# Storing expert 6's result in nine parts on one queue instead of three parts on two

## The chip, the cores and the metric

The kernel runs on one core of one Trainium2 chip. The metric is device time in microseconds (us): the time of one execution of the program, taken as the median of several runs. The core has TensorE (matrix products), VectorE (DVE in the profile), ScalarE (ACT), GpSimd (POOL) and SyncE (SP). GpSimd, SyncE and ScalarE can issue DMAs, each on a queue of its own; 16 DMA engines carry out what is in these queues.

## The reference

Eight experts, each with its own 256 x 512 input and its own two-layer network:

```
x  [8, 256, 512]    w1 [8, 512, 2048]    b1 [8, 2048]
                    w2 [8, 2048, 512]    b2 [8, 512]        all float32

h   = max(x @ w1 + b1, 0)          # per expert, 256 x 2048
out = h @ w2 + b2                  # per expert, 256 x 512, float32
```

The output is 8 x 256 x 512 float32, 4.19 MB. The weights are 67 MB; they are cast to float16 while they are loaded.

## The kernel before

**Loads.** GpSimd issues all weight loads, one DMA of 128 partitions per expert and matrix (`load_w1`, `load_w2`; the last two experts' `w2` in two halves), in a fixed order that the list `ring` writes out. Three buffers each hold `w1` and `w2`; a load waits until the expert that used its buffer is done. SyncE loads the inputs of experts 0 and 1 at the start, as two DMAs of 128 rows of 4 KB; GpSimd loads the others.

**Products.** The loop over `s` runs `first_product(s)` and, three experts behind, `second_product(s - 3)`. The first gives h transposed, 16 blocks of 128 rows, which ScalarE takes out of PSUM with bias and ReLU. The second accumulates two PSUM tiles `po` of 128 x 512, one for the even and one for the odd ones of the 256 output rows, and starts with a product of ones and `b2`.

**Results.** In `store`, VectorE copies the first tile out of PSUM (line 156) and ScalarE the second (line 157), both into an SBUF tile of 128 partitions. Partition p holds the output rows 2p and 2p + 1, so each partition is one contiguous piece of 4 KB in SBUF and in HBM. Below, "row" means such a 4 KB piece. Three ways lead to HBM:

- Experts 0 to 3 share one tile (`GROUPS`), stored by one GpSimd DMA of 2 MB; experts 4 and 5 share another, stored by one of 1 MB. `flush` (line 140) issues both late, after the last weight loads. They are called group 0's and group 4's store here.
- Expert 7 is stored by one SyncE DMA of 128 rows, after its two copies.
- Expert 6 is stored in the parts that the table `PARTS` gives: first row, last row, and whether ScalarE (true) or SyncE (false) issues it. This is line 164, in the loop at the end of `store`.

**Waiting.** A DMA raises a semaphore of its own when it has landed. The framework gives each DMA of SyncE and ScalarE the next of eight semaphores in turn, and gives GpSimd's another eight. At the end of the program SyncE waits for all of them, one instruction after the other (shown under line 261).

Of the kernel before, what the change touches and what calls it, by code (L numbers as in the profile page):

```python
# [10 lines left out]
def kernel(  # L11
# [12 lines left out]
    E, T, H = x.shape  # L24
# [12 lines left out]
    HALVED = (E - 2, E - 1)  # L37


    PARTS = {E - 2: ((0, 25, False), (25, 121, True), (121, 128, False))}  # L40
    nXF32 = 2
    X_LOADS = {2: 2, 4: 4}

# [98 lines left out]
    def store(e, po):  # L142
# [16 lines left out]
        if e in group_of:  # L159
            if e == first + n - 1:  # L160
                pending[first] = (dst, out_sb)
            return
        for p0, p1, scalar in PARTS.get(e, ((0, P, False),)):
            (nc.scalar if scalar else nc.sync).dma_start(out=dst[p0:p1], in_=out_sb[p0:p1])
# [101 lines left out]
```

## Time and profile before

| what | time |
|---|---|
| median of 3 runs | 181.49 us (181.38 to 181.49) |
| span of the profiled execution, first to last instruction | 179.7 us |
| that execution's own device time | not recorded apart from the span |
| difference between the median and the span | 1.8 us |
| TensorE busy | 129.1 us, 72% of the span |
| GpSimd's DMA queue, share of the 16 engines' time | 96.6% |
| second products of experts 5, 6, 7 start | 149.5, 158.7, 166.3 us |
| group 0's store issued / landed | 148.3 / 175.1 us |
| group 4's store issued / landed | 159.7 / 177.5 us |
| expert 6's store issued | 166.4 us |
| expert 7's last copy ends, its store is issued | 173.9 us |
| expert 7's store landed | 178.8 us |

The profile is of one execution. Its times are counted from the first instruction. A DMA instruction on an issuing engine's queue takes a fraction of a microsecond; the data moves afterwards on the DMA engines, and the time to landing is the time from the start of the issue to the last increment of the semaphore. The page counts a DMA's packets: one per piece of data and one for each engine's increment of the semaphore. The column PEq, SPq and so on means an engine's sequencer or DMA queue.

### The profile page before, as it was taken

The numbers are of one execution on the slowest core, as the hardware profiler recorded it, in microseconds if no ns is written. First come the engines' busy times: TensorE is split into PE (matmuls) and PEld (weight loads), VectorE is DVE, ScalarE is ACT, GpSimd is POOL, SyncE is SP. The second block draws the span as 40 slices with busy tenths as digits, with TensorE's granted clock in tenths as the row PEclk, the third lists the DMA queues.
The fourth block names the chain that finished last, engine by engine and source line by source line (L and its number), as shares of the span: only waits on it lengthen the run. The fifth ranks groups of instructions, "written<-read, shape, count | busy, mean of one in ns | idle before, by whom it ended". The sixth has DMA issues, their size and how long they took to land.

```text
span 179.7 us, 1958 instructions
## 1 busy us (share of the span) xinstructions
PE 129.1 (72%) x784; PEld 85.8 (48%) x784; DVE 88.0 (49%) x125; ACT 70.2 (39%) x151; POOL 13.1 (7%) x28
## 2 busy tenths in 40 slices
PE   0005099969595970899969597969497887999950
PEld 0004079969592320795369244844195332433420
DVE  0999942987000199999999998003200020301010
ACT  0000459969593022483099005950586020020010
POOL 7000002120201010001010001000200021010000
PEclk9999999999998798589999889999999996999996
DMA  5999999999999999999999999999999999999996
GB/s 216 251 226 199 233 212 197 233 224 193 228 230 192 221 233 215 197 230 230 204 208 230 219 193 233 226 193 222 230 215 197 233 206 204 223 212 215 335 420 250
DMA packets 3829, 40.56 MB, mean 226 GB/s; under 512 B 461, under 2 KB 477, under 8 KB 1133
## 3 DMA queue, kind: packets, MB, share of 16 engines
q0 software_dynamic: 3232, 38.35, 96.6%
q1 hardware_dynamic: 476, 1.70, 2.4%
q10 hardware_dynamic: 112, 0.39, 0.5%
q8 instruction: 6, 0.10, 0.2%
q14 instruction: 3, 0.02, 0.0%
HBM read 71.39 MB, written 4.19 MB: 421 GB/s over the span
## 4 chain that ended last, share of the span: by engine, by line
DMA 66%; PE 26%; POOL 2%; another core or an unknown queue 1%; issue 1%; ACT 0%; POOLq 0%
DMA w1sb<-in_w_dram 44%; DMA w2sb<-in_w_dram 22%; PE po L178 18%; PE ph L121 8%; PE po L171 1%; POOL w1sb L84 1%; ACT out L157 0%; POOL x L76 0%; POOL b_sb L192 0%; POOL b_rows L196 0%; POOLq L250 0%
## 5 line engine op out<-in xcount | busy, mean ns | idle before, releaser
L121 PE MATMUL ph<-xT,w1sb 128*128 128x256 f16 x512 | 63.6, 289 | 34.8 <-DMA w1sb<-in_w_dram 23.9
L121 PEld LDWEIGHTS <-w1sb 128*128 128x128 f16 x512 | 59.0, 147 | 40.3 <-DMA w1sb<-in_w_dram 32.6
L178 PE MATMUL po<-w2sb,hT 128*128 128x512 f16 x256 | 61.4, 402 | 9.4 <-DMA w2sb<-in_w_dram 9.4
L112 DVE STREAM_TRANSPOSE xT<-x 32x256 f16<-32x256 f16 (+1 forms) x64 | 53.1, 889 | 25.6 <-DMA x<-in_x_dram 18.7
L128 ACT ACTIVATE hT<-ph,b1T 128x256 f16<-128x256 f32 x128 | 56.2, 474 | 13.6 <-PE ph L121 13.4
L178 PEld LDWEIGHTS <-hT 128*128 128x128 f16 x256 | 25.9, 102 | 44.7 <-issue 19.3
L156 DVE COPY out<-po 32x512 f32<-32x512 f32 (+2 forms) x22 | 15.1, 688 | 54.0 <-PE po L178 53.8
L157 ACT COPY out<-po 32x512 f32<-32x512 f32 (+2 forms) x22 | 12.7, 579 | 69.7 <-PE po L178 69.5
L109 DVE STREAM_TRANSPOSE xT<-x 32x256 f16<-32x256 f16 x32 | 14.0, 436 | 0.5
L93 POOL DMA_DIRECT2D w2sb<-in_w_dram x10 | 5.3, 534 | 72.8 <-PE po L178 72.8
L128 ACT ACT_TABLE_LOAD x1 | 1.3, 1283 | 20.5 <-DVE b1T L208 20.5
L84 POOL DMA_DIRECT2D w1sb<-in_w_dram x8 | 4.5, 558 | 63.2 <-PE ph L121 62.4
L171 PE MATMUL po<-b_sb,ones 1*128 1x512 f16 x16 | 4.8, 379 | 0.0
L208 DVE STREAM_TRANSPOSE b1T<-b_rows 32x512 f32<-32x512 f32 x4 | 4.1, 1035 | 0.1
L201 DVE CAST x<-x 128x1024 f16<-128x1024 f32 x2 | 1.5, 757 | 3.3 <-DMA x<-in_x_dram 3.3
L140 POOL DMA_DIRECT2D out_dram<-out x2 | 1.1, 542 | 10.9 <-ACT out L157 10.9
L171 PEld LDWEIGHTS <-ones 1*128 1x128 f16 x16 | 0.9, 92 | 2.1 <-issue 2.1
L76 POOL DMA_DIRECT2D x<-in_x_dram x2 | 1.1, 552 | 0.0
L197 DVE MEMSET ones<- 1x128 f16 x1 | 0.2, 165 | 0.8 <-PEq L250 0.8
L196 POOL DMA_DIRECT2D b_rows<-in_b_dram x1 | 0.5, 515 | 0.0
L192 POOL DMA_DIRECT2D b_sb<-in_b_dram x1 | 0.5, 513 | 0.0
L250 POOL MEMSET const-float32-0.0<- 128x1 f32 x1 | 0.1, 99 | 0.2 <-issue 0.2
(3 smaller groups left out, 0.3 us busy)
## 6 DMA issues: line engine op xcount, KB each, us to landing
w1sb<-in_w_dram POOLq DMA_DIRECT2D x8, 2048.0 KB, 34.5
w2sb<-in_w_dram POOLq DMA_DIRECT2D x6, 2048.0 KB, 46.8
w2sb<-in_w_dram POOLq DMA_DIRECT2D x4, 1024.0 KB, 24.0
out_dram<-out POOLq DMA_DIRECT2D x1, 2048.0 KB, 26.8
x<-in_x_dram SPq DMA_DIRECT2D x2, 512.0 KB, 3.9
x<-in_x_dram POOLq DMA_DIRECT2D x1, 1024.0 KB, 30.8
out_dram<-out POOLq DMA_DIRECT2D x1, 1024.0 KB, 17.8
x<-in_x_dram POOLq DMA_DIRECT2D x1, 512.0 KB, 24.0
```

What stands on the lines that cost most here:

```text
L84: ordered(nc.gpsimd.dma_start(out=w1_sb[e], in_=w1[e].rearrange("(p kc) m -> p kc m", kc=nKC)))
L93: ordered(nc.gpsimd.dma_start(out=w2_sb[e][:, lo : lo + half], in_=src[:, lo : lo + half]))
L109: nc.vector.transpose(out=out[:, :, g, :, 0, :], in_=block[:, :, :, 0, :])
L112: nc.vector.transpose(out=out[:, tb, g], in_=block[:, tb])
L121: ordered(nc.tensor.matmul(out=ph, lhsT=w1_sb[e][:, kc, :].rearrange("p (q j) -> p q j", j=nJ)[:, :, j], rhs=xT[e][:, kc, :], start=(kc == 0),
L128: nc.scalar.activation(out=hT[e][:, j, :].rearrange("p (tb k i) -> p tb k i", tb=nTB, k=split), in_=ph.rearrange("p (tb i k) -> p tb k i", ...
L156: nc.vector.tensor_copy(out=out_sb[at : at + rows, k * nTB, :], in_=po[0][part])
L157: nc.scalar.copy(out=out_sb[at : at + rows, k * nTB + 1, :], in_=po[1][part])
L171: ordered(nc.tensor.matmul(out=t, lhsT=ones1, rhs=b2_sb[0:1, e * H : (e + 1) * H], start=True, stop=False,))
L178: ordered(nc.tensor.matmul(out=po[tb], lhsT=hT[e][:, j, tb * P : (tb + 1) * P], rhs=w2_sb[e][:, j, :], start=False, stop=(j == nJ - 1),))
L201: nc.vector.tensor_copy(out=t, in_=x32[e])
L208: nc.vector.transpose(out=b1T[b * B : (b + 1) * B, nB - 1 - b : nB - 1 - b + nJ * B], in_=b1_rows.rearrange("r (i j) -> r j i", j=nJ),)
```

## The change

Expert 6's store is cut differently, and SyncE issues all of it. Before, SyncE issued rows 0 to 24 and 121 to 127, and ScalarE rows 25 to 120. After, SyncE issues nine parts in order, of 64, 15, 13, 11, 9, 7, 5, 3 and 1 rows. The rows, their bytes and their places in HBM are the same. Nothing else in the program text differs; one added line moves all later line numbers by one.

```diff
-    PARTS = {E - 2: ((0, 25, False), (25, 121, True), (121, 128, False))}
+    cuts = (0, 64, 79, 92, 103, 112, 119, 124, 127, 128)
+    PARTS = {E - 2: tuple((lo, hi, False) for lo, hi in zip(cuts, cuts[1:]))}
```

## The prediction

> **What bounds the kernel now.** I read the page's DMA parts first, then the timeline and the stretches of the last 14 us, then the waits of SP. The 16 DMA engines are busy from the first load to the end, and the page gives each queue's packets:
>
> ```profile
> q0 software_dynamic: 3232, 38.35, 96.6%
> q1 hardware_dynamic: 476, 1.70, 2.4%
> q10 hardware_dynamic: 112, 0.39, 0.5%
> q8 instruction: 6, 0.10, 0.2%
> ```
>
> Queue 0 is GpSimd's, 1 SyncE's, 10 ScalarE's, 8 fetches instructions. Queue 10 carried the 96-row part: 112 = 96 rows of 4 KB + 16 four-byte increments of its semaphore, one per engine used. Queue 1 carried two loads of 128 rows, the last store, and the 25 and 7 rows: 3 x 144 + 32 rows leaves 12 increments, 5 + 7. So 25 rows ran on five engines with five rows each, 7 rows on seven with one each. The six fetches are one 16 KB packet each, at 36.5, 53.5, 83.9, 105.7, 134.8 and 159.6 us.
>
> The timeline of the tail (start, duration, operation):
>
> ```profile
> 166.21 7.08 PE L178 MATMUL po<-w2sb,hT 128*128 128x512 f16 x32
> 166.40 7.91 SPq L164 DMA_DIRECT2D out_dram<-out  x3
> 166.40 0.38 ACTq L164 DMA_DIRECT2D out_dram<-out  x1
> ...
> 173.33 0.59 ACT L157 COPY out<-po 128x512 f32<-128x512 f32 x1 [6.96 <-PE po L178]
> ```
>
> Expert 6's store starts at 166.40, expert 7's when its last copy ends at 173.92. The stretches (DMA's busy share is the column before GB/s):
>
> ```profile
> 173.90:175.80 1.90, 0.00 (x0) 0.00 (x0) 0.00 (x0) 0.02 (x1) 0.00 (x0) 1.00 0.98 408
> 175.80:177.00 1.20, 0.00 (x0) 0.00 (x0) 0.00 (x0) 0.00 (x0) 0.00 (x0) 0.87 0.95 399
> 177.00:177.50 0.50, 0.00 (x0) 0.00 (x0) 0.00 (x0) 0.00 (x0) 0.00 (x0) 0.50 0.93 377
> 177.50:178.00 0.50, 0.00 (x0) 0.00 (x0) 0.00 (x0) 0.00 (x0) 0.00 (x0) 0.50 0.70 287
> 178.00:178.45 0.45, 0.00 (x0) 0.00 (x0) 0.00 (x0) 0.00 (x0) 0.00 (x0) 0.50 0.30 118
> 178.45:179.70 1.25, 0.00 (x0) 0.00 (x0) 0.00 (x0) 0.00 (x0) 0.00 (x0) 0.50 0.00 0
> ```
>
> There is no idle stretch between the start of expert 7's store and the end: the engines are full until 177, then 0.70 of 16 is eleven. Five engines run out near 177.3, eleven near 178.3. The end is set by **the DMA engine with most bytes left**, not by the store's latency.
>
> **The sum per engine.** The trace has no engine numbers for packets, but in the tail each engine's next packet starts a fixed step after the last: 607 ns after 16 KB of a store, 305 after 8 KB, 155 after 4 KB, 6 after an increment. By these steps the packets fall into 16 chains. Each serves 8 packets of group 0's store, 8 of group 4's, its rows of expert 6 and 8 rows of expert 7. With six rows of expert 6 that is 4,869 + 2,445 + 932 + 1,242 ns and increments, 9,506 ns from its first 16 KB packet, and the chains end where this says, within 4 ns (one within 21):
>
> ```
> engines              first 16 KB packet (us)              rows  last packet (us)
> 0-4 (25 and 7 rows)  167.59 167.79 167.80 167.95 167.96   12    178.06 to 178.41
> 5, 6 (7 rows)        168.448, 168.587                      7    178.12, 178.25
> four others          168.779 168.787 168.810 168.917       6    178.29 to 178.43
> five others          167.53 to 168.03                      6    177.04 to 177.54
> ```
>
> Six chains start 0.9 us late. Followed back through the loads by the same method, 168.448 holds the fetch at 36.5, 168.587 that at 53.5, 168.779 that at 83.9, 168.810 that at 105.7; the last two fetches I can't place with confidence. The first two being engines 5 and 6, I take the fetches to go to engines 5, 6, 7, 8, 9, 10 in turn.
>
> **The change.** ScalarE loses one DMA issue of 0.38 us; it then waits 6.96 us for TensorE, so the gain is nothing. SyncE gains seven issues. Its rows last 0.36 to 0.60 us, with some 0.05 between, so the first eight parts take at most 5.2 us, 166.40 to 171.6. Expert 7's store waits for its copies until 173.92 anyway: TensorE's second product hides the issues with 2.3 us to spare. Without that cover the store would be issued up to 4.5 us later, seven issues of 0.65.
>
> *Rows per engine.* 25, 7, 96 and 128 rows took 5, 7, 16 and 16 engines, so a part takes the largest divisor up to 16 of its rows, and the five engines of the 25 rows are among the seven of the 7 (their chains hold one more row), so each part starts from the same first engine: 64 gives four each, every smaller part one row to as many engines as it has rows. Engines 0 to 15 then have 12, 11, 11, 10, 10, 9, 9, 8, 8, 7, 7, 6, 6, 5, 5 and 4 rows. At 155 ns a row and 6 ns an increment:
> - 5: 9 rows, +0.33 us on its 178.12: 178.45. 6: 9 rows, 178.25 becomes 178.59.
> - 7, 8: 8 rows, +0.335: 178.62 and 178.65. 9, 10: 7 rows, +0.17: 178.47 and 178.60.
> - 0: twelve rows as before, six more increments: at most 178.45. All others end earlier.
>
> The last packet moves from 178.43 to 178.65: **+0.22 us**. If 7 and 8 are the two latest, +0.33; if neither is late, engine 6 alone still gives +0.16. Only if fetches lie elsewhere is it below: then engine 0 decides, at best 178.1 to 178.45, -0.14 (with 178.29 on engine 1) to +0.02.
>
> [...]
>
> *A new wait.* The built order of SyncE in the changed kernel has waits that the diff does not show. Its DMAs use eight semaphores in turn; the two loads took the first two. The seventh and eighth part reuse those, satisfied since 5.5 us. The ninth part (1 row) reuses that of the 64 rows and waits for their landing; expert 7's store, queued behind it, reuses that of the 15 rows and waits for theirs. Nobody but the end waits behind the store. Price: the 64 rows go out one per turn beside GpSimd's queue, as the 96 did. On the latest chain (168.917) the rows start at 170.75, 171.51, 172.28, 173.04; the increment at 173.80 and that of the 15 rows at 174.57. From an increment's packet to the semaphore event the 96 rows took 0.36 to 0.60 us: 174.4 and 175.1. The 1-row issue in between (0.4 to 0.65) ends by 175.05. So expert 7's store is issued near 175.2 instead of 173.94, **1.2 us later**. Does it cost? The page's x loads on empty engines started their first packet 1.03 us after the issue; expert 7's rows before came at most 1.85 us after, on the engine first empty. They arrive between 176.2 and 177.0. The late engines are busy with queues 0 and 1 until 1.24 us before their end, the deciding one until 177.4. So I take **0**; the cover is 0.4 to 1.2 us. Engines 11 to 15 run dry earlier, but with 1.24 us of rows from 177.0 they still end at 178.25.
>
> *The closing waits.* SyncE ends with one wait after another:
>
> ```profile
> L261 SPq EVENT_SEMAPHORE  x6: 28/28/28, 177.6 to 177.9; - x6
> ```
>
> These six, already satisfied, start 0.062 us apart (177.559 to 177.867). Before, the wait for expert 7's store was the last of the row (178.80, 0.02 after the landing at 178.78). In the built order after, that store's semaphore is the fourth of eight hardware ones; four more waits follow it. All are satisfied, but each is stepped through: 4 x 0.062 = **+0.25 us**. Bounds: 0.11 (28 ns each) to 0.25.
>
> **Sum.** 0.22 + 0 + 0.25 = +0.47 us. The profiled span of 179.68 becomes 180.15; the page has no other time of that execution, so I take the 1.81 us between span and the median of 181.49 as unchanged: 181.96, +0.26%, said as 182.0 us. A measurement of this kernel can tell about 0.2% (0.36 us) from no change.
>
> **Rivals.**
> 1. *Not slower: the fetches don't load engines 5 to 8 in the timed runs.* From the point where no late engine has more rows than before, the row term is -0.14 to +0.02 instead of +0.22; with the closing waits at 0.11 to 0.25 the time is 181.46 to 181.76. For it: only two engines are placed by their rows. Against: late chains 168.448 and 168.587 have the seventh part's row, and three timed runs agree within 0.11 us.
> 2. *Expert 7's store becomes the bound* through the new wait. If it kept its 4.84 us from issue (173.94) to landing (178.78), 175.2 would land at 180.0: +1.25, and +0.25 of closing waits, 183.0 us. It decides once the rows arrive after 177.4: an issue past 175.6 with the long delay of 1.85, past 176.4 with the short. Against: most of the 4.84 was queue 0's backlog, which goes on draining meanwhile. A slip of 0.3 to 0.8 us is likelier: 182.2 to 182.8.
> 3. *The parts don't spread as I read.* If 15 and 9 rows went to five and three engines, engine 0 would carry four rows more than before, 0.62 us: 182.4. Nothing in the counts of 25, 7, 96 and 128 rows speaks for it.
>
> **Chances.** Forecast 0.62, of which 0.56 above the bound and 0.06 within; rival 1 0.15 (0.10 within, 0.03 above, 0.02 faster); rivals 2 and 3 0.15, all above; something unseen 0.08 (0.05 faster, 0.02 same, 0.01 slower). Together faster 0.07, same 0.18, slower 0.75. The range 181.6 to 182.5 holds the forecast's bounds (+0.16 + 0.11 to +0.33 + 0.25), half of rival 1 and the small slips of 2, and leaves out the rest.
>
> **What would show it.** In the profile after: queue 10 gone; queue 1 with 3 x 144 + 128 rows + 80 increments = 640 packets; SyncE's last DMA at 175.0 to 175.4; the last packet at 178.6 to 178.8; four satisfied waits after the last landing; the span 180.1 to 180.3. An idle gap on the DMA between 176 and 177.5 beyond a few engines, or a last DMA after 175.6, means rival 2. A last packet at or before 178.43 means that the late engines are not 5 to 8, and the forecast is wrong.

## The result and the profile after

The changed kernel takes 182.56 us (median of 4 runs, 182.53 to 182.61) beside 181.49 for the kernel before: +1.07 us by the medians, a ratio of 1.0051 (95% interval 1.0038 to 1.0063), which is +0.93 us. Measured a second time it took 182.42 beside 181.75: +0.67 us, 1.0034 (1.0022 to 1.0047). The prediction's sum was +0.47 us and its range 181.6 to 182.5 us: the first median lies 0.06 us above that range, the second inside it. The profiled execution of the first measurement took 182.55 us; its span of 180.76 us is 1.09 us longer than before.

The queues of the changed kernel, first by the page (packets, MB, share of the 16 engines' time):

```profile
q0 software_dynamic: 3232, 38.35, 96.0%
q1 hardware_dynamic: 640, 2.10, 3.2%
q8 instruction: 6, 0.10, 0.2%
```

Queue 10 is gone and queue 1 has the 640 packets that the counting rule asked for: 3 x 144 + 128 rows + 80 increments. The increments of the nine parts' semaphores came 16, 15, 13, 11, 9, 7, 5, 3 and 1 at a time. Followed by the prediction's steps (607, 305, 155 and 6 ns), the packets fall into 16 chains with 12, 11, 11, 10, 10 and so on down to 4 rows of expert 6, and 8 of expert 7, as the sum had them. Engine 0 below is the one with most.

Which chains are late is not as the sum had it. Engines 5 and 6 are, and begin group 0's store at 168.53 and 168.55 us. The other four late ones, which begin it at 169.22 to 169.42, have six or five rows of expert 6: they are engines 11 to 14. Engines 7 to 10, which the prediction put among the late ones, begin it at 167.61 to 167.99 and end by 178.07. In five more profiles with nine parts (the change again, apart in HBM alone, four more loads, and both with the last store by ScalarE) the late chains are again engines 5 and 6 and four of the engines 9 to 14, never 7 and 8.

The timeline of the tail (start, duration, operation):

```profile
164.71 3.63 PE L179 MATMUL po<-w2sb,hT 128*128 128x512 f16 x16
164.89 10.90 SPq L165 DMA_DIRECT2D out_dram<-out  x10
169.75 3.61 PE L179 MATMUL po<-w2sb,hT 128*128 128x512 f16 x16 [1.42 <-DMA w2sb<-in_w_dram]
173.40 0.59 ACT L158 COPY out<-po 128x512 f32<-128x512 f32 x1 [8.54 <-PE po L179]
```

In this execution TensorE ran expert 5's second product in 7.07 us instead of 8.66, so expert 6's copies ended 1.5 us earlier and SyncE began its issues at 164.89. Expert 7's copies did not: the second half of its product waited 1.42 us for the last weights, and its last copy ended at 173.99, as before (173.92). SyncE's DMA instructions under the store's line, shortest, median and longest in ns, first after, then before:

```profile
L165 SPq DMA_DIRECT2D out_dram<-out x10: 350/1062/1672, 164.9 to 174.9; - x10
```

```profile
L164 SPq DMA_DIRECT2D out_dram<-out x3: 358/360/596, 166.4 to 173.9; - x3
```

The first three issues took 0.54, 0.62 and 0.35 us; the next six 1.05, 1.49, 1.67, 1.66, 1.08 and 1.09. They ended at 174.78 and expert 7's store was issued at 174.90, 0.9 us after its last copy.

The stretches of the tail (DMA's busy share is the column before GB/s):

```profile
173.90:175.80 1.90, 0.00 (x0) 0.00 (x0) 0.00 (x0) 0.09 (x1) 0.00 (x0) 1.00 0.98 405
175.80:177.00 1.20, 0.00 (x0) 0.00 (x0) 0.00 (x0) 0.00 (x0) 0.00 (x0) 0.62 0.98 386
177.50:178.00 0.50, 0.00 (x0) 0.00 (x0) 0.00 (x0) 0.00 (x0) 0.00 (x0) 0.50 0.85 344
178.00:178.45 0.45, 0.00 (x0) 0.00 (x0) 0.00 (x0) 0.00 (x0) 0.00 (x0) 0.50 0.69 282
178.45:179.30 0.85, 0.00 (x0) 0.00 (x0) 0.00 (x0) 0.00 (x0) 0.00 (x0) 0.50 0.23 92
```

No idle stretch again, but 0.69 of the engines are busy from 178.00 to 178.45 (0.30 before), and packets go on until 179.26 (178.43 before). The stretch where this begins shows busy engines that move less, in the changed kernel and then in the kernel before:

```profile
172.50:174.50 2.00, 0.86 (x5) 0.20 (x2) 0.00 (x0) 0.59 (x1) 0.00 (x0) 1.00 0.95 354
```

```profile
172.50:174.50 2.00, 0.79 (x4) 0.18 (x2) 0.00 (x0) 0.59 (x1) 0.00 (x0) 1.00 0.94 393
```

The busy share is the same, 354 GB/s stand against 393. Read packet by packet, the kernel before has no row in the tail that takes over 0.18 us. The changed kernel has many. Seven rows of the 15-row part moved together from 172.53 on. By the counts of rows on their chains they are those of engines 0, 3, 4, 5 and 6, one of 1 and 2, and one of 7 and 8. They took

```
seven rows of the 15-row part, in the order in which they started (us)
start      172.53  172.56  172.81  172.86  172.93  172.95  173.11
duration    0.291   1.105   0.719   0.492   0.762   0.391   0.288
```

instead of 0.159. The other eight rows of the same part took 0.159: two that moved some 0.5 us earlier, one that moved at 173.71, and five that moved at the same time as the seven, from 172.73 to 172.88. Over the whole tail the packets took 4.6 us of engine time more than their size asks for. I call this sum the **excess**: what the packets of 4, 8 and 16 KB took beyond 159, 309 and 611 ns, counted from 168.5 us on where it is over 20 ns. It is 0.0 before. Of the 4.6 us, 3.4 lie on the eight small parts, 0.8 on expert 7's rows, 0.3 on GpSimd's packets and 0.1 on the 64 rows.

The closing waits that start after the last landing (179.615), with the end of the program's barrier among them:

```profile
L262 SPq EVENT_SEMAPHORE  x5: 28/28/28, 179.6 to 179.9; - x5
```

They start at 179.631, 179.690, 179.752, 179.811 and 179.873: the store's own and four behind it. From the last landing to the end of the span it takes 1.15 us (0.89 before).

So the 1.09 us of the span are 0.83 to the last packet (178.43 to 179.26) and 0.25 of closing waits. The chains that ended last are those of engines 5 and 6, at 179.26 and 179.09, with 0.70 and 0.56 us of long rows; without these they would have ended at 178.55 and 178.53. The latest engine with no long row ended at 178.78, so the long rows cost the end 0.47 us. That engine is 13 or 14. It has five rows of expert 6, where the late engines had six or seven before, but began group 0's store at 169.42, where the latest one before began it at 168.92. Why it did is open. Such differences between two profiles, of up to 0.5 us, have to be kept in mind wherever last landings are compared below.

### The profile page after: what moved, and what is told of

Read it like the earlier page. It is cut to its first block, busy times and chain, and to the rows that moved or that the text cites. A ratio compares the mean times of both kernels' runs of the same rounds, so it can differ in the third digit from the quotient of the medians.

```text
span 180.8 us, 1964 instructions
## 1 busy us (share of the span) xinstructions
PE 128.8 (71%) x784; PEld 86.1 (48%) x784; DVE 88.0 (49%) x125; ACT 70.2 (39%) x151; POOL 13.1 (7%) x28
## 4 chain that ended last, share of the span: by engine, by line
DMA 55%; PE 32%; ACT 3%; another core or an unknown queue 3%; POOL 2%; issue 1%; POOLq 0%
DMA w1sb<-in_w_dram 43%; PE po L179 16%; PE ph L122 15%; DMA w2sb<-in_w_dram 12%; ACT out L158 3%; PE po L172 1%; POOL w1sb L85 1%; ACT hT L129 1%; POOL b_rows L197 0%; POOL b_sb L193 0%; POOL x L77 0%; POOL w2sb L94 0%; POOLq L251 0%
## 5 line engine op out<-in xcount | busy, mean ns | idle before, releaser
L122 PE MATMUL ph<-xT,w1sb 128*128 128x256 f16 x512 | 64.8, 292 | 34.4 <-DMA w1sb<-in_w_dram 21.6
L122 PEld LDWEIGHTS <-w1sb 128*128 128x128 f16 x512 | 59.7, 147 | 40.3 <-DMA w1sb<-in_w_dram 31.8
L179 PE MATMUL po<-w2sb,hT 128*128 128x512 f16 x256 | 60.0, 394 | 10.1 <-DMA w2sb<-in_w_dram 10.1
```

The lines of the kernel that those rows point to most:

```text
L122: ordered(nc.tensor.matmul(out=ph, lhsT=w1_sb[e][:, kc, :].rearrange("p (q j) -> p q j", j=nJ)[:, :, j], rhs=xT[e][:, kc, :], start=(kc == 0),
L179: ordered(nc.tensor.matmul(out=po[tb], lhsT=hT[e][:, j, tb * P : (tb + 1) * P], rhs=w2_sb[e][:, j, :], start=False, stop=(j == nJ - 1),))
```

## The experiments

The theory after this reading: the increase is rows per engine (+0.1 to +0.4), rows slowed because neighbouring partitions are read at the same time (+0.3 to +0.7), and closing waits (+0.25). Rivals: many small transfers are slow whatever their places; neighbours in HBM rather than in SBUF are to blame; the place of expert 7's store behind SyncE's issues sets the end.

The measurements together. "Before" is the median of the kernel before on the same chip, the ratio goes with its 95% interval, excess and last landing are those of one profiled execution (before: 0.0 and 178.78).

| kernel | us | before | ratio | excess us | last landing |
|---|---|---|---|---|---|
| the change | 182.56 | 181.49 | 1.0051 (1.0038 to 1.0063) | 4.6 | 179.62 |
| the change again | 182.42 | 181.75 | 1.0034 (1.0022 to 1.0047) | 4.2 | 179.34 |
| six input loads | 185.19 | 181.58 | 1.0184 (1.0141 to 1.0227) | 4.0 | 182.58 |
| parts apart in SBUF and HBM | 182.05 | 181.58 | 1.0024 (1.0001 to 1.0047) | 1.3 | 179.87 |
| apart in HBM alone | 182.52 | 181.58 | 1.0043 (1.0022 to 1.0064) | 6.4 | 179.50 |
| apart in SBUF alone | 182.25 | 181.58 | 1.0027 (1.0005 to 1.0048) | 1.2 | 179.77 |
| four more loads | 182.26 | 181.61 | 1.0025 (1.0012 to 1.0038) | 4.9 | 179.56 |
| apart, last store by ScalarE | 181.89 | 181.61 | 1.0012 (0.9997 to 1.0027) | 1.7 | 179.07 |
| neighbours, last store by ScalarE | 182.25 | 181.75 | 1.0030 (1.0015 to 1.0045) | 2.8 | 179.46 |
| one part of 128 rows | 181.92 | 181.61 | 1.0000 (0.9986 to 1.0013) | 0.0 | 179.32 |
| short rows | 181.51 | 181.61 | 0.9986 (0.9971 to 1.0) | 3.1 | 178.88 |
| eight parts of neighbours | 182.05 | 181.57 | 1.0024 (1.0013 to 1.0034) | 6.4 | 179.32 |
| eight parts apart | 182.09 | 181.57 | 1.0026 (1.0015 to 1.0037) | 0.4 | 179.15 |

**Closing waits, first try.** The two input loads become six, so that expert 7's store gets the eighth semaphore and no wait follows its own.

```diff
-        nc.sync.dma_start(out=x32[e], in_=x[e].rearrange("(p tb) h -> p tb h", tb=nTB))
+        for lo, hi in ((0, 32), (32, 64), (64, 128)):
+            nc.sync.dma_start(out=x32[e][lo:hi], in_=x[e].rearrange("(p tb) h -> p tb h", tb=nTB)[lo:hi])
```

> The nine parts as in the changed kernel; only the two input loads at the start are cut into six pieces, so that expert 7's store gets the eighth hardware semaphore instead of the fourth and its closing wait is the last of the row. The reuse stays the same: the 1-row part waits for the 64 rows, expert 7's store for the 15 rows. If the four closing waits behind it cost 0.25 us, the time falls from 182.56 to 182.3 us and the wait for the last landing is followed by no other wait on a DMA. Rival: the end is set by something else after the last landing; then it stays at 182.5 to 182.6.

Measured: +3.6 us, for a reason outside the question. Start of the profile (SyncE's loads and the first cast of the input):

```profile
0.73 3.06 SPq L192 DMA_DIRECT2D x<-in_x_dram  x6
13.57 0.69 DVE L204 CAST x<-x 128x1024 f16<-128x1024 f32 x1 [12.59 <-DMA x<-in_x_dram]
```

The first cast is at 13.57 us instead of 4.26: six issues take until 3.8 us, GpSimd issues the first weights from 1.24 us on, the cast waits 12.59 us for the input, and everything is 3 to 4 us later. The time says nothing of the closing waits; only the trace's end does: the last landing at 182.58 is followed by its own wait alone.

**Closing waits, second try.** Four small loads behind the two large ones do the same and disturb nothing.

```diff
+    spare = singles.tile([16, 4 * P], fp32)
+    for i in range(4):
+        nc.sync.dma_start(out=spare[:, i * P : (i + 1) * P], in_=x[2, 0:16, 0:P])
```

> The nine parts as in the changed kernel; behind the two input loads SyncE issues four more loads of 16 x 512 bytes into a tile that nobody reads. They only take four semaphores, so that expert 7's store gets the eighth and its closing wait is the last; the reuse is as in the changed kernel. If each of the four closing waits behind that store costs 0.06 us, this is 0.25 us faster than the changed kernel (182.56), 182.3 us. If nothing after the last landing counts, 182.5 to 182.6. The span from the last landing to the end should fall from 1.16 to 0.9 us.

Measured: 1.0025 (+0.65 us by the medians), against 1.0034 and 1.0051 for the change. The wait for the last store starts at 179.58, 0.016 us after the landing, and no other follows; the span ends 0.90 us after the landing, as before, not 1.15. The long rows stayed (excess 4.9). By the trace the closing waits are worth what the prediction gave them; the times do not show it by themselves, since the intervals overlap.

**Small parts apart, in SBUF and HBM.** The 64 rows stay; the eight small parts have their sizes, but each takes every fourth row. The edit, shortened:

```diff
-        for p0, p1, scalar in PARTS.get(e, ((0, P, False),)):
-            (nc.scalar if scalar else nc.sync).dma_start(out=dst[p0:p1], in_=out_sb[p0:p1])
+        nc.sync.dma_start(out=dst[0:64], in_=out_sb[0:64])
+        for c, lo, hi in ((0, 0, 15), (1, 0, 13), (2, 0, 11), (3, 0, 9), (3, 9, 16), (2, 11, 16), (1, 13, 16), (0, 15, 16)):
+            rows = slice(64 + 4 * lo + c, 64 + 4 * (hi - 1) + c + 1, 4)
+            nc.sync.dma_start(out=dst[rows], in_=out_sb[rows])
```

> The same nine sizes on the same queue, but the 64 rows of the eight small parts are taken every fourth row, so that the rows which several engines move at once lie 16 KB apart in HBM and four partitions apart in SBUF. Theory A (rows that are neighbours slow each other when several engines move them at once): the long packets of the 15-row part (up to 1.1 us in place of 0.16) go, the last packet comes near 178.6, and the time falls by 0.5 to 0.7 us to 181.9 to 182.1. Theory B (many small parts on one queue stall an engine by themselves): long packets remain, 182.4 to 182.7.

Measured: 182.05 us, eight runs at 181.91 to 182.21 and four at 182.59 to 183.03. The excess falls from 4.6 to 1.3 us, and 0.5 of this lies on 16 KB packets of group 0's store. But the profiled execution, one of the four longer ones at 182.83 us, has another fault:

```profile
166.44 0.56 SPq L166 DMA_DIRECT2D out_dram<-out  x1
167.04 10.05 SPq L170 DMA_DIRECT2D out_dram<-out  x8
177.22 0.37 SPq L164 DMA_DIRECT2D out_dram<-out  x1
```

```profile
176.50:177.50 1.00, 0.00 (x0) 0.00 (x0) 0.00 (x0) 0.00 (x0) 0.00 (x0) 1.00 0.33 127
177.50:178.00 0.50, 0.00 (x0) 0.00 (x0) 0.00 (x0) 0.00 (x0) 0.00 (x0) 0.54 0.02 8
178.00:178.45 0.45, 0.00 (x0) 0.00 (x0) 0.00 (x0) 0.00 (x0) 0.00 (x0) 0.50 0.88 355
```

TensorE's product of expert 5 took 8.75 us here, so the issues began at 166.44. They ran until 177.09, 3.1 us past expert 7's last copy (173.95), and the store behind them was issued at 177.22. From 177.50 to 178.00 the engines are at 0.02: this is the idle gap that rival 2 named. The 15 rows had landed at 175.04, so it was not the new wait that held the store, but the issues in front of it.

**Apart on one side only.** To keep neighbours on one side and not on the other, the hidden rows of expert 6 are reordered when ScalarE writes h, so that another output row lands in each partition; those lines are left out here. First HBM apart (SBUF neighbours), then SBUF apart (HBM neighbours):

```diff
+            hbm = slice(64 + 4 * lo + c, 64 + 4 * (hi - 1) + c + 1, 4)
+            sbuf = slice(64 + 16 * c + lo, 64 + 16 * c + hi)
+            nc.sync.dma_start(out=dst[hbm], in_=out_sb[sbuf])
```

> The small parts' rows are neighbours in SBUF, as in the changed kernel, and 16 KB apart in HBM. To bring them there, expert 6's hidden columns are written in another order, in two ScalarE instructions in place of one for each of its 16 blocks (more ScalarE time near 130 us, where ScalarE mostly idles). If neighbours in SBUF are what slows the rows: long packets, 182.4 to 182.7 us. If neighbours in HBM: none, 181.9 to 182.1. Theory B: long packets in any case.

```diff
+            hbm = slice(64 + 16 * c + lo, 64 + 16 * c + hi)
+            sbuf = slice(64 + 4 * lo + c, 64 + 4 * (hi - 1) + c + 1, 4)
+            nc.sync.dma_start(out=dst[hbm], in_=out_sb[sbuf])
```

> The reverse: the small parts' rows lie four partitions apart in SBUF and are neighbours in HBM, by the same reordering. If neighbours in HBM are what slows the rows: long packets, 182.4 to 182.7 us. If neighbours in SBUF: none, 181.9 to 182.1. Theory B: long packets in any case.

Measured: with SBUF neighbours the excess is 6.4 us (4.4 of it on rows), and the 15-row part has rows of 0.36 to 0.82 us again; with SBUF apart it is 1.2 us (0.7 on rows) and no row is over 0.41. In these two profiles it is the SBUF side that goes with the long rows. The times (1.0043 and 1.0027, overlapping) do not part the two: in the profile of the second, expert 7's store was again issued late, at 177.12, behind issues of up to 2.29 us.

**Expert 7's store out of SyncE's queue.** Parts apart as above, and the last store by ScalarE. It then has the eighth semaphore, waits for no part and stands behind no issue.

```diff
-            nc.sync.dma_start(out=dst, in_=out_sb)
+            nc.scalar.dma_start(out=dst, in_=out_sb)
```

> As e2_both_apart (rows four apart), and expert 7's store issued by ScalarE after its own last copy, so that it stands neither behind SyncE's issues nor behind a reused semaphore, and its closing wait is the last. Left over is only the number of rows per engine. Theory: 0.2 us over the kernel before in all runs (181.7 to 181.85 where that is 181.55), with no second group of times as e2 had, and the store issued at 173.9. Rival (the engines' rows are worth more than 155 ns each, or two queues cost more than one): 182.0 or more, as e2's faster group.

```profile
L164 ACTq DMA_DIRECT2D out_dram<-out x1: 375/375/375, 173.8 to 173.8; - x1
```

Measured: issued at 173.81, landed at 179.07, 1.0012 (0.9997 to 1.0027): +0.2 us, and no change lies within the interval too. Little but the rows per engine is left here (excess 1.7). Engines 5 and 6, with under 0.05 us of long rows, end at 178.46 and 178.51; the chain that ended last, at 178.71, is engine 13 or 14 with 0.35 us of long packets. Then the same with the nine parts of the change, neighbours again:

> The changed kernel with expert 7's store on ScalarE's queue: no closing wait behind its own, no wait for the 15 rows, no queueing behind SyncE's issues. The nine parts stay of neighbouring partitions. It differs from the kernel with the small parts' rows four partitions apart and the last store by ScalarE in the neighbours alone, which stood at +0.2 us (ratio 1.0012). Theory (neighbouring partitions slow the rows, and the slow rows fall on an engine that sets the end): rows +0.2, slow rows +0.3 to +0.7, together +0.5 to +0.9 us, 182.1 to 182.5 us; long rows again at seven engines of the 15-row part. Rival (what hurts is the last store's place behind the small parts' issues, and the slow rows are made up for): +0.2, 181.8 us, as with the rows apart.

Measured: 1.0030 (1.0015 to 1.0045), last landing 179.46, excess 2.8 us. The difference to the kernel with the rows apart is 0.0018 x 181.7 = 0.33 us, and 0.39 us in the last landings of the two profiles. The theory's range was met, but the intervals overlap, and the landings differ for another reason: the chain that ended last, engine 5 or 6, carries only 0.18 us of long rows and began group 0's store at 168.91, where engines 5 and 6 began it at 168.41 and 168.51 with the rows apart.

**The change again**, beside it:

> The changed kernel itself, beside the runs of the kernel before on the same chip as the next one. Theory (rows per engine +0.1 to +0.2 us, slow rows from neighbouring SBUF partitions +0.3 to +0.7, four more closing waits +0.25): 0.65 to 1.15 us above the kernel before, 182.3 to 182.8 us if that stays at 181.6. Rival (the slow rows of the profiled run were chance; what is left is the sum of the prediction): +0.47, 182.1.

Measured: +0.67 us, at the low end of the theory and nearer to the rival's +0.47 than the first measurement was. The long rows were there again (excess 4.2 us), so they are no chance. What they cost at the end differs: the last landing is 0.56 us after that of before, not 0.83. The chain that ended last, at 179.00, is engine 1 or 2 with 0.70 us of long rows; engine 5 or 6 ended at 178.83 with none. So the long rows cost the end 0.18 us here and 0.47 in the first profile. SyncE's issues, and expert 7's last copy:

```profile
165.04 10.76 SPq L165 DMA_DIRECT2D out_dram<-out  x10
173.20 0.58 ACT L158 COPY out<-po 128x512 f32<-128x512 f32 x1 [8.19 <-PE po L179]
```

The nine parts' issues ran until 175.33 and the store behind them was issued at 175.44, 1.7 us after its copy. The 15 rows had landed at 174.41, so the issues held it.

**One part.** The table is emptied, so that expert 6's store is one DMA of 128 rows.

```diff
-    PARTS = {E - 2: ((0, 25, False), (25, 121, True), (121, 128, False))}
+    PARTS = {}
```

> Expert 6's store as one DMA of 128 rows on SyncE: eight rows on every engine, one increment, no neighbours at a time, no reused semaphore, no closing wait behind the last store. By the sum per engine the six late chains get 1 to 2 rows more than before: the latest from 178.43 to 178.73, +0.3 us, 181.85 where the kernel before is 181.55. Rival (rows per engine don't set the end): 181.5 to 181.6.

Measured: 181.92 beside 181.61 by the medians, a ratio of 1.0000 (0.9986 to 1.0013). The profile's last landing is 0.54 us later than before; whether the time is, stays unclear. The excess is 0.0: 128 rows on one DMA, eight neighbours to an engine, are not slow.

**Short rows.** The eight small parts store only 512 bytes of each row; the rest of those rows is not stored.

> The nine parts of the changed kernel, but the eight small ones move 512 bytes of each row in place of 4 KB; the rest of those rows isn't stored. What sets SyncE's pace (issues of 1.0 to 1.7 us from the fourth part on)? If the queue takes only a few transfers or descriptors per engine and moves on as the engines take turns with GpSimd's queue, the issues stay as long, because a turn lasts as long as GpSimd's packet. If it is the bytes under way, they fall to 0.4 to 0.6 us and expert 7's store is issued right after its copy, 173.9 to 174.0.

```profile
L167 SPq DMA_DIRECT2D out_dram<-out x10: 251/873/2300, 166.4 to 176.2; - x10
```

Measured: 0.9986 (0.9971 to 1.0). An eighth of the bytes, and the longest issue is 2.30 us: the length of an issue does not follow the bytes of its part. The last store was issued at 176.21. There are long packets here too, an excess of 3.1 us, and none of it on the short rows, which take 27 to 29 ns each. Four 16 KB packets of group 0's store, from 171.26 to 171.44, take 0.83 to 1.06 us in place of 0.61, and rows of the 64-row part up to 0.73, nearly all of it before the first short row moves at 173.45. So the neighbours in the small parts are not the only thing that makes packets long. What the other is, no run here isolates.

**Neighbours or small transfers.** Eight parts of 16 rows, the last store by ScalarE. Every engine gets one row of each part. The two kernels have the same parts, rows per engine, issues and semaphores, and differ in the partitions that a part takes: 16 in a row, or every eighth. The lines of both:

```diff
+        for c in range(8):
+            rows = slice(16 * c, 16 * c + 16)        # neighbours
+            rows = slice(c, P - 7 + c, 8)            # apart (the other kernel)
+            nc.sync.dma_start(out=dst[rows], in_=out_sb[rows])
```

> Expert 6's store in eight SyncE parts of 16 rows, each of 16 neighbouring partitions, expert 7's store by ScalarE. Every engine gets one row of each part, so the rows per engine are those of the single part of 128 (8 each), and only 7 increments per engine come on top (0.04 us). Neighbours meet in all 128 rows instead of 64. Theory (rows of neighbouring SBUF partitions that move at the same time slow each other): rows of up to 1 us again, an excess of more than the 4 to 5 us of engine time of the nine parts, the last landing 0.4 to 1.5 us after that of the next kernel, 0.7 to 2 us above the kernel before. Rival (the excess comes from many small transfers on one queue, whatever their places): the same excess and the same time as the next kernel.

> The same eight parts of 16 rows, but part c takes the rows c, c + 8, c + 16 and so on: 8 partitions apart in SBUF and 8 rows apart in HBM. Number of parts, rows per engine and issues are those of the kernel with neighbours. Theory: rows near 0.16 us as in the single part, an excess under 2 us of engine time, 0.2 to 0.5 us above the kernel before (the single part stood 0.0 to 0.3 above). Rival (many small transfers): excess and time as in the kernel with neighbours.

The pages' rows of queue 1, neighbours first, then apart:

```profile
q1 hardware_dynamic: 544, 1.57, 2.6%
```

```profile
q1 hardware_dynamic: 544, 1.57, 2.3%
```

The same packets and bytes take 2.6% instead of 2.3% of the engines' time. SyncE's issues are alike (shortest, median, longest, in ns):

```profile
L169 SPq DMA_DIRECT2D out_dram<-out x8: 356/1281/1805, 164.9 to 172.4; - x8
```

```profile
L169 SPq DMA_DIRECT2D out_dram<-out x8: 552/1309/1631, 164.8 to 172.9; - x8
```

Two stretches of the tail are not, again neighbours first:

```profile
172.50:174.50 2.00, 0.46 (x3) 0.00 (x0) 0.00 (x0) 0.58 (x1) 0.00 (x0) 1.00 0.88 315
177.50:178.00 0.50, 0.00 (x0) 0.00 (x0) 0.00 (x0) 0.00 (x0) 0.00 (x0) 0.50 0.75 303
```

```profile
172.50:174.50 2.00, 0.64 (x3) 0.10 (x1) 0.00 (x0) 0.59 (x1) 0.00 (x0) 1.00 0.93 383
177.50:178.00 0.50, 0.00 (x0) 0.00 (x0) 0.00 (x0) 0.00 (x0) 0.00 (x0) 0.50 0.51 205
```

With neighbours 315 GB/s move where 383 move without, and the rest is made up after 177.5. The excess is 6.4 us against 0.4, rows last up to 1.03 us against 0.32. Number and size of the transfers are the same, so it is the places; and with the two kernels apart on one side only, it is the places in SBUF. So neighbouring partitions read by several engines at once are a cause of long rows, shown in one profile of each kernel. They are not the only one, as the short rows showed.

The **time** did not follow: 1.0024 and 1.0026. My expectation of 0.7 to 2 us for the neighbours was wrong. Of the 16 chains, with the rows apart ten end at 177.4 to 177.9 and six, as many as there are late engines, at 178.3 to 178.8. With neighbours five end at 177.5 to 177.8 and eleven at 178.2 to 178.95, and the worst five, all early engines, carry 0.75 to 1.18 us of long packets. So the early engines had some 0.9 us of slack, and the long rows used it up and little more. The two chains that end last, at 178.95 and 178.87, are late engines with 0.55 and 0.47 us of long rows. That the last landing is only 179.32 against 179.15 is in part chance: the late engines begin group 0's store by 168.94 in that profile, and as late as 169.12 in the other. Even that difference vanished in the time, since the kernel with rows apart had its eighth part landing at 179.13 and then stepped through five waits until 179.45, the other until 179.39.

No kernel measured here is faster than the one before and stores everything.

## Why the prediction was right and where it fell short

**Right in direction and in the last term; the first term's mechanism held for two engines.** The eight small parts go to as many engines as they have rows (15, 13, 11, 9, 7, 5, 3 and 1 increments), and by the chains the two rows more on engines 5 and 6 moved their ends. For engines 5 and 6 the sum had 178.45 and 178.59: they end at 178.46 and 178.51 with the rows apart and the last store by ScalarE, and at 178.53 and 178.55 in the first profile if their long rows are taken off. The closing waits were +0.25 in both profiles of the change, four starts of 0.06 each, and were gone with the eighth semaphore. The sum priced the parts themselves at 6 ns an increment, and no more than that shows: the eight parts apart land at 179.15, the single part with the same rows per engine at 179.32.

**The late engines.** "I take the fetches to go to engines 5, 6, 7, 8, 9, 10 in turn" was wrong. Engines 7 and 8, which gave the sum its 178.65, were late in none of the six profiles that were followed; in the first they ended at 177.90 and 178.07. By the prediction's own working, 178.59 for engine 6 and +0.16 were left of the row term. That the latest undisturbed chain ended at 178.78, near the bound of 178.76, is luck: it is an engine with fewer rows than before, whose loads ended later. The +0.2 us that was left with the rows apart and the last store by ScalarE fits +0.16 as well as +0.22, and no change too.

**The step that failed: "at 155 ns a row".** The chains of before gave that price for rows that move one per engine in places far apart, and I used it for parts that put neighbouring partitions on neighbouring engines. The mechanism was missing, not a size: with the neighbours' rows up to 1.1 us, the last packet moved by 0.83 us in the first profile and the last landing by 0.56 in the second, where the term had 0.22. What the long rows cost the end is 0.47 us by the chains of the first profile and 0.18 by those of the second. Their share in the time is not shown: between the two kernels that differ in them and have the last store by ScalarE it is 0.33 us with overlapping intervals, and between the two kernels of eight parts nothing. By the chains the difference is slack. The change gives engines 0 to 4 ten to twelve rows, so that they end close behind the late ones, gives two of the late ones nine, and lands its long rows on these. In the eight equal parts the early engines have eight rows and room for them.

Which of the neighbours' rows were slowed is not explained. If the rows of a part go to the engines in order, the seven long rows above (0.288 to 1.105 us) are partitions 64, 67 to 70, one of 65 and 66, and one of 71 and 72. The other one of partitions 65 and 66 started at 172.78 and took 0.159, and so did 73 and 74, within 0.03 us of each other. The parts with little excess took every fourth row (1.2 to 1.7 us) or every eighth (0.4), and rows apart took 0.159 nearly throughout. So the places in SBUF agree with which kernels had the large excess but not with which rows were long, and what in SBUF makes the rows wait stays open.

**The issues.** "0.36 to 0.60 us each, at most 5.2 us, 2.3 us to spare" was wrong: the first eight took 8.75 us. They did not stay behind TensorE's product. In the first profile they began 1.5 us earlier than before, and expert 7's store was issued at 174.90, inside the bound of 175.2 that the new wait had set (the 15 rows landed at 174.83). In the second it was issued at 175.44, past that bound. Neither profile has a gap on the engine that ended last, so this cost nothing there. Where they began at 166.4 (the kernel with the rows apart) they ended 3.1 us past the copies, and rival 2 came true, by another road than the new wait: the store's wait was already satisfied, its turn was not there. The prediction's own sentence for that case, a cover gone at 4.5 us later, was the one to price. Neither profile of the change has such an idle gap, and whether some of its runs have it stays open.

**Rivals 1 and 3.** Rival 3 can be dropped: the parts spread as read. Rival 1 was half right: engines 7 and 8 were not late, but 5 and 6 were, and these alone kept the row term above nothing.

## What to carry to other kernels

Before a store is split into small parts, look at which partitions move at the same time: with parts of 16 neighbouring partitions the engines moved 315 GB/s from 172.50 to 174.50 (busy share 0.88) where the same rows taken every eighth moved 383 (0.93). Here that did not change the time by itself. By the chains, slowed transfers fell mostly into slack there: early engines took up to 1.18 us of long packets on some 0.9 us of slack, and the times were 1.0024 and 1.0026. In the first profile of the nine parts 0.70 us of long rows lay on an engine that set the end, and cost it 0.47 us. So a cut that balances the engines to the last row can also take away the room for such accidents. Before engines are balanced by which of them are late, more than one profile should say which these are. And a transfer that ends the kernel should not stand in a queue behind a row of small issues: behind SyncE's issues expert 7's store was issued 0.9 us after its last copy in the first profile of the change and 3.3 us with the rows apart, on ScalarE's queue within 0.1 us, and with the last semaphore no closing wait followed its own.

## What the runs showed of the hardware

- In the changed kernel, with GpSimd's queue at 88.9% of the 16 engines' time from 164.9 to 174.9 us, SyncE's first three DMA instructions took 0.54, 0.62 and 0.35 us and the next six 1.05 to 1.67. The longest took 1.63 and 1.81 us in the two kernels of eight parts, 2.29 with SBUF alone apart, and 2.30 with 512 bytes of each row. ScalarE's one issue at 173.81, in the kernel with the rows apart, took 0.375 us.
- Rows of neighbouring SBUF partitions, read by several engines at once, took up to 1.1 us instead of 0.159; neighbours in HBM that lay four partitions apart in SBUF took at most 0.41. Some other packets grew long with no such neighbours moving (0.83 to 1.06 us for 16 KB instead of 0.61, with short rows).
- In six profiles with nine parts, six of the 16 engines begin group 0's store later (168.39 to 169.42 us) than the other ten (by 168.27): 5 and 6 each time, and four of 9 to 14 that are not the same in all of them.
- One satisfied wait in SyncE's closing row takes 0.06 us, and which semaphore a DMA gets decides how many follow it: four behind the fourth of eight (0.25 us, the changed kernel), none behind the eighth (four more loads).
